# Longer rows in the prelude, one chain of side work for context keys and values, and full-width output units in a hybrid backbone layer

## The chip, the cores and the metric

The kernel runs on one core of one Trainium2 chip. The metric is the device time of one execution in microseconds (us); the time of a version is the median over its runs. The profile is of one execution and has its own time.

## The reference

One layer of a bidirectional backbone: 1024 latent tokens `x` and 256 context tokens `ctx`, width 2048, float32. Both are normalised and modulated with vectors computed from `c` and `c_ctx`, projected by `w_in` (10256 columns) and go through two groups of heads: eight HGRN2 heads (gated linear recurrence) and four mLSTM heads (matrix memory, with a short convolution on queries and keys). The context's final states seed the latent's scans.

```python
mod_x = silu(c) @ w_mod + b_mod                  # 3 sections: shift, scale, gate
mod_c = silu(c_ctx) @ w_mod + b_mod
u_ctx = modulate(ctx, shift_c, scale_c) @ w_in
y_ctx, ctx_states = mix(u_ctx, False, states0, *lp)   # only the states are used
u_x = modulate(x, shift_x, scale_x) @ w_in
y_x, _ = mix(u_x, True, ctx_states, *lp)
x = layer_norm(ALPHA * x + gate_x * (y_x @ w_out), ln_g, ln_b)
```

## The kernel before

Every product of the projections is taken with both factors split into a rounded part and a rest (`hi`, `lo`), so that one product is three matmuls, `xh·hi`, `xh·lo` and `xl·hi` (`mm3`, L222-232). ScalarE (ACT) makes `whi` from the loaded `wraw`, VectorE (DVE) makes `wlo` (L217, L218; in the deep ring of the last output groups L201, L202). SyncE's queue (SP) brings the weights.

The program is written as one stream of projection units, with side work in generators. After some 24 matmuls a unit calls `tick()` (L73), which moves each generator on by one step, to its next `yield`; a `yield n` asks for n ticks until the next step. `finish` (L81) runs a generator to its end on the spot. So a generator's steps stand in TensorE's instruction order between the matmuls of the units, and what is not stepped through by ticks stands in a row behind them. A matmul that waits holds up all behind it on its engine.

The stages that matter here:

- **Prelude** (L301-354). The shift and scale sections of `w_mod` are taken in eight eighths of 256 columns. `adaln_cols` (L356) loads each as eight tiles `am_raw` of two k-tiles, two transfers each with rows of 1 KB (L366), and multiplies with a stationary operand of 32 columns that fills one of four column groups (`o = 32 * (k % 4)`, L372), all in one PSUM bank. The sums are copied to `mod_rows` (L375), gathered with `comb` (L382) and added to the bias (`modc`); `ln_kp` (L431) transposes two k-tiles of the normalised context (L439) and modulates them. Between the eighths stand the context projections of keys and values of mLSTM heads 0 to 2, two k-tiles at a time, 256 columns a head. Six PSUM banks hold them until the end.
- **Context phase** (`phase_ctx`, L582). The context's gates (L588, L589), keys 3 and values 3, then for each pair of HGRN2 heads forget gates forward and backward and the input (`ctx_unit`). Side work: `ctx_k` (convolution over padded copies, transposes L673), `ctx_v`, `ctx_f` (decayed keys `c_kd` L722, each followed at once by its transposes L726), `ctx_i`, and normalising the latent tokens in four quarters (`lat_load`, `lat_gen`). The third and fourth quarters share their buffers (`hh1*`, `hl1*`) with the context, so they come after the last context projection, together with the latent gates (`gates_mm`, L575, L576) and three early mLSTM units.
- **mLSTM and HGRN2 heads**, some 2000 us, which the change hardly touches.
- **Output** (`phase_out`, `out_group` L1250). The heads' results go through DRAM (`d_y`) and are read back as `yh`, `yl` by GpSimd's queue (POOL, L1244). Row tiles of 128 tokens are taken in three groups, 4 + 2 + 2. A unit is 1024/n columns wide: 256 for the first group, 512 for the others. `evac` multiplies a finished bank with the gate (L1274), adds `ALPHA` times a piece of `x` that POOL loaded (L1275) and takes statistics (L1276). `out_norm` normalises a group and stores it from ACT's queue (L1320). Four row buffers `res` serve all groups. The PSUM pools (five `pj`, two `mx` and one `mx3` banks) are open from the start to the end, so output matmuls of the first unit are placed among the last head's instructions.

Of the kernel before, what the change touches and what calls it, by code (L numbers as in the profile page):

```python
# [38 lines left out]
class Body:  # L39
# [46 lines left out]
    def run(self):  # L86
        tc = self.tc
        with tc.tile_pool(name="const", bufs=1) as self.cp, \
                tc.tile_pool(name="hts", bufs=1) as self.hp, \
                tc.tile_pool(name="wts", bufs=1) as self.wp, \  # L90
                tc.tile_pool(name="psp", bufs=5, space=PSUM) as self.psp, \
                tc.tile_pool(name="psm", bufs=2, space=PSUM) as self.psm, \
                tc.tile_pool(name="dr", bufs=1, space=DRAM) as self.dp:
            self.setup()
            with tc.tile_pool(name="wgp", bufs=1) as self.gp:
                with tc.tile_pool(name="ph1a", bufs=1) as self.mp:
                    self.prelude()
                with tc.tile_pool(name="ph1", bufs=1) as self.mp:
                    self.phase_ctx()
            with tc.tile_pool(name="ph2", bufs=1) as self.mp:  # L100
                self.phase_mlstm()
            with tc.tile_pool(name="ph3", bufs=1) as self.mp:
                self.phase_hgrn()
            with tc.tile_pool(name="ph4", bufs=1) as self.mp:
                self.phase_out()


    def setup(self):
# [3 lines left out]
        nc.gpsimd.dma_start(out=self.comb, in_=a["k_comb"])  # L112
# [71 lines left out]
    def weights(self, src, cols, k0, nk, deep=False, ahead=True, pool=None):  # L184
# [3 lines left out]
        with self.tc.high_priority() if ahead else nullcontext():  # L188
# [15 lines left out]
            if pool is None:  # L204
                raw = self.wp.tile([P, nk, wd], F32, tag="wraw", bufs=2, name=self.nm("wraw"))
            else:
                raw = pool.tile([P, nk, wd], F32, tag="praw", bufs=6, name=self.nm("wraw"))
# [81 lines left out]

    def cht(self, k):  # L290
# [10 lines left out]
    def prelude(self):  # L301
# [3 lines left out]
        with self.tc.high_priority():  # L305
            nc.scalar.dma_start(out=cr[0:16], in_=a["c"].rearrange("o (r p) -> (o r) p", p=P))
            nc.scalar.dma_start(out=cr[16:32], in_=a["c_ctx"].rearrange("(r p) -> r p", p=P))
            nc.scalar.dma_start(out=self.ident, in_=a["k_ident"])
# [8 lines left out]

        self.wg = self.gp.tile([P, 16, 32], F32R, name="wg")
        gr = mp.tile([P, 16, 16], F32, name="wg_raw")
        nc.scalar.dma_start(out=gr, in_=a["w_in"][:, CG:CG + 16].rearrange("(k p) n -> p k n", p=P))  # L320
        hi, lo = self.wg[:, :, 0:16], self.wg[:, :, 16:32]
        nc.scalar.copy(hi, gr)
        nc.vector.tensor_tensor(out=lo, in0=gr, in1=hi.bitcast(F32), op=ALU.subtract)
        units = [self.pj([P, 2, 256]) for _ in range(5)]
        units.append(self.psm.tile([P, 2, 256], F32, tag="mx3", bufs=1, name=self.nm("mx")))
        rows = self.adaln_cols(0, ch)
        self.vectors()

        self.hth, self.htl = [None, None], [None, None]
        self.cth = [self.hp.tile([P, 2, 256], F32R, tag=f"hh1{k}", name=self.nm("cth")) for k in range(8)]  # L330
        self.ctl = [self.hp.tile([P, 2, 256], F32R, tag=f"hl1{k}", name=self.nm("ctl")) for k in range(8)]
        xa = []
        for i in range(2):
            xt = [self.hp.tile([P, 1024], F32, tag=f"hh0{i * 2 + s}", name=self.nm("cx")) for s in range(2)]
            for s in range(2):
                nc.scalar.dma_start(out=xt[s], in_=a["ctx"][i * P:(i + 1) * P, s * 1024:(s + 1) * 1024])
            self.ln_norm(xt)
            xa.append(xt)
        for e in range(9):
            if 0 < e < 8:  # L340
                rows = self.adaln_cols(e, ch)
            for h in range(3 if e else 0):
                k0 = 2 * e - 2
                parts = self.weights(a["w_in"], [(CMK + h * 256, 256), (CMV + h * 256, 256)], k0, 2, ahead=False,
                                     pool=mp)
# [1051 lines left out]
```

## Time and profile before

| | |
|---|---|
| median of 3 runs | 2912.41 us (2912.31 to 2923.12) |
| the profiled execution's own time | 2913.54 us |
| its span | 2911.7 us |
| mean granted TensorE clock | 0.989 of full |
| TensorE, VectorE, ACT, POOL busy | 97%, 53%, 32%, 13% of the span |

The span is the stretch that the profile covers; the own time of that execution is 1.8 us longer. "PE" is TensorE, "PEclk" the share of its full clock that was granted; "idle before, releaser" names what ended the idle time ahead of an instruction on its engine. The time bought or lost on an engine other than TensorE shows only where TensorE waits for it.

### The profile page before, as it was taken

What the parts mean: (1) busy time and instruction counts of PE and PEld (TensorE: products, weight loads), DVE (VectorE), ACT (ScalarE), POOL (GpSimd) and SP (SyncE); (2) the same over time, 40 slices, a digit from 0 to 9 for tenths busy, and PEclk for the clock granted to TensorE, in tenths of its full rate; (3) what the DMA queues carried; (4) which work ended last, traced back from release to release, by engine and by line L of the source; (5) the groups of instructions that cost most, each with busy time, mean ns of one, the idle gap of its engine ahead of it and who ended that gap; (6) DMA issues with size and microseconds to landing.
All of it is one profiled execution on the core that took longest, in us unless ns stands there. A gap on an engine that the chain in (4) does not pass through costs nothing.

```text
span 2911.7 us, 47253 instructions
## 1 busy us (share of the span) xinstructions
PE 2823.9 (97%) x19337; PEld 2408.6 (83%) x19337; DVE 1543.7 (53%) x3017; ACT 931.6 (32%) x1654; POOL 368.4 (13%) x550
## 2 busy tenths in 40 slices
PE   6899999999999999999999999999999999999998
PEld 3798976988887898789778888888888888899876
DVE  3387657563835655474625352534435353544776
ACT  1275446341233123222323231323223232322332
POOL 1011011031112103201310101011010101310111
PEclk9999999999999999999999999999999999999999
DMA  9945642124223322332241111121111212853784
GB/s 331 348 153 167 190 120 73 50 55 116 80 64 82 109 73 72 103 94 77 62 115 48 53 45 54 44 60 53 45 54 44 61 37 60 256 183 120 243 301 172
DMA packets 331960, 325.12 MB, mean 112 GB/s; under 512 B 16640, under 2 KB 285216, under 8 KB 329696
## 3 DMA queue, kind: packets, MB, share of 16 engines
q1 hardware_dynamic: 296976, 243.04, 27.8%
q0 software_dynamic: 30336, 69.15, 8.2%
q10 hardware_dynamic: 4432, 9.91, 0.9%
q8 instruction: 152, 2.49, 0.3%
q14 instruction: 64, 0.52, 0.1%
HBM read 289.00 MB, written 33.05 MB: 111 GB/s over the span
## 4 chain that ended last, share of the span: by engine, by line
PE 73%; DVE 4%; issue 2%; DMA 2%; POOL 1%; ACT 1%; DVEq 0%; POOLq 0%; ACTq 0%; SPq 0%
PE pj L226 16%; PE pj L228 16%; PE pj L227 16%; PE pj L230 5%; PE pj L232 5%; PE pj L231 5%; PE mx L1108 2%; PE mx L951 1%; PE mx L956 1%; PE mx L1189 1%; DVE m_acc L862 1%; PE mx L949 1%; DMA yl<-d_y 1%; DMA m_bc<-d_rows 1%; POOL m_rs L938 0%
## 5 line engine op out<-in xcount | busy, mean ns | idle before, releaser
L226 PE MATMUL pj<-hh,whi 128*128 128x512 f32 x2304 | 923.5, 401 | 0.7 <-ACT m_pad L784 0.7
L228 PE MATMUL pj<-hh,wlo 128*128 128x512 f32 x2304 | 900.6, 391 | 0.0
L227 PE MATMUL pj<-hl,whi 128*128 128x512 f32 x2304 | 899.6, 390 | 0.0
L218 DVE TENSOR_TENSOR wlo<-wraw,whi 128x512 fp32r<-128x512 f32 x556 | 390.4, 708 | 669.4 <-ACT whi L217 561.8
L217 ACT CAST whi<-wraw 128x512 fp32r<-128x512 f32 x556 | 340.3, 619 | 861.1 <-PE pj L227 533.5
L228 PEld LDWEIGHTS pj<-hh,wlo 128*128 128x128 f32 x2304 | 433.0, 188 | 93.2 <-issue 0.4
L226 PEld LDWEIGHTS pj<-hh,whi 128*128 128x128 f32 x2304 | 433.3, 188 | 92.7 <-issue 2.5
L227 PEld LDWEIGHTS pj<-hl,whi 128*128 128x128 f32 x2304 | 433.6, 188 | 86.5
L230 PE MATMUL pj<-whi,yh 128*128 128x256 f32 (+1 forms) x768 | 245.9, 320 | 4.4 <-DVE res L1274 4.4
L231 PE MATMUL pj<-wlo,yh 128*128 128x256 f32 (+1 forms) x768 | 245.6, 320 | 0.0
L232 PE MATMUL pj<-whi,yl 128*128 128x256 f32 (+1 forms) x768 | 245.4, 320 | 0.1
L862 DVE SCALAR_TENSOR_TENSOR m_acc<-m_pad,cwt,m_acc 128x512 f32<-128x512 f32 x256 | 188.6, 750 | 3.5
L230 PEld LDWEIGHTS pj<-whi,yh 128*128 128x128 f32 x768 | 147.0, 191 | 15.0 <-DVE res L1274 4.8
L232 PEld LDWEIGHTS pj<-whi,yl 128*128 128x128 f32 x768 | 146.9, 191 | 10.4 <-DMA yl<-d_y 0.3
L231 PEld LDWEIGHTS pj<-wlo,yh 128*128 128x128 f32 x768 | 146.9, 191 | 10.2
L230 PE MATMUL pj<-whi,hh 128*128 128x256 f32 x512 | 147.2, 287 | 0.9 <-ACT m_pad L784 0.9
L232 PE MATMUL pj<-whi,hl 128*128 128x256 f32 x512 | 144.9, 283 | 0.0
L231 PE MATMUL pj<-wlo,hh 128*128 128x256 f32 x512 | 144.8, 283 | 0.0
L1220 POOL TENSOR_TENSOR h_ss<-h_ss,nhalf 128x4 f32<-128x4 f32 x16 | 16.6, 1036 | 804.0 <-DVE h_ss L1219 804.0
L228 PE MATMUL pj<-cth,wlo 128*128 128x256 f32 x384 | 112.4, 293 | 5.3 <-DVE wlo L218 5.3
L1092 ACT COPY h_km<-h_kk 128x512 f32<-128x512 f32 x112 | 74.6, 666 | 125.9 <-DVE h_kk L1145 98.4
L226 PE MATMUL pj<-cth,whi 128*128 128x256 f32 x384 | 114.6, 298 | 0.0
(313 smaller groups left out, 3937.9 us busy)
## 6 DMA issues: line engine op xcount, KB each, us to landing
wraw<-in_w_in_dram SPq DMA_DIRECT2D x222, 512.0 KB, 3.8
wraw<-in_w_out_dram SPq DMA_DIRECT2D x96, 512.0 KB, 4.3
am_raw<-in_w_mod_dram SPq DMA_DIRECT2D x128, 256.0 KB, 6.0
wraw<-in_w_mod_dram SPq DMA_DIRECT2D x32, 512.0 KB, 3.6
d_y<-yhl POOLq DMA_DIRECT2D x64, 256.0 KB, 3.9
wraw<-in_w_in_dram SPq DMA_DIRECT2D x48, 256.0 KB, 6.0
xt<-in_x_dram SPq DMA_DIRECT2D x8, 1024.0 KB, 6.7
m_bc<-d_rows POOLq DMA_DIRECT2D x64, 128.0 KB, 3.4
```

Source lines behind the costliest of these rows:

```text
L217: nc.scalar.copy(hi, r)
L218: nc.vector.tensor_tensor(out=lo, in0=r, in1=hi.bitcast(F32), op=ALU.subtract)
L226: mm(o, hi, xh, start=start, stop=False, skip_group_check=True)
L227: mm(o, hi, xl, start=False, stop=False, skip_group_check=True)
L228: mm(o, lo, xh, start=False, stop=stop, skip_group_check=True)
L230: mm(o, xh, hi, start=start, stop=False, skip_group_check=True)
L231: mm(o, xh, lo, start=False, stop=False, skip_group_check=True)
L232: mm(o, xl, hi, start=False, stop=stop, skip_group_check=True)
L862: V.scalar_tensor_tensor(out=acc, in0=src, scalar=wc, in1=acc, op0=ALU.mult, op1=ALU.add)
L949: nc.tensor.matmul(po[:, 0:257], w, v1[:, c, :], start=True, stop=False)
L1092: nc.scalar.copy(view(km, 0, [[2 * B, 512 // (2 * B)], [B, 2], [1, B]]), view(kk, g * 512, [[2 * B, 512 // (2 * B)], [T + B, 2], [1, B]]))
L1108: nc.tensor.matmul(p3[q0:q0 + TW, c, :], kms[c // 4][:, cc + q0:cc + q0 + TW], rhs(c * P, j), start=True, stop=True, skip_group_check=True)
```

## The change

**Prelude.** The sections are taken in four quarters of 512 columns. A tile `am_raw` holds one k-tile of both sections, so its rows are 2 KB. A quarter is four groups `g` of four k-tiles (`adaln_mm`); within a group `j` is the column group, and the two sections go to two PSUM banks. Each of the quarters 1 to 3, and a fifth round without loads, has a context step (`ctx_first`) behind each group: keys of all four heads for one k-tile (24 matmuls) and values of heads 0 and 1, 512 columns wide (6 matmuls). Small loads (`ident`, the context, the gates' weights) move from ACT's queue to POOL's. The context rows now lie in one half of the buffers of latent quarters three and four.

**Context phase.** The four finished key banks are copied to `c_sk` at once and convolved from there without pads. Keys and values of heads 0 and 1 and keys 2 and 3 are one chain. Values 2 and 3 are one unit of 512 columns at the third head pair (`ctx_pair`). Latent quarters two and three and the load of four are one chain among the head pairs, and only `lat_gen(3)` comes behind them. `ctx_f` makes both decayed keys, then yields, then transposes both.

**Output.** All units are 512 wide. The heads' PSUM pools close first and the output has a pool of eight banks. `res` is loaded with whole rows of `x` by ACT's queue; `evac` writes `res = ALPHA * res + p * gb` through a tile `o_t`. The scratch memory of POOL's transfers is halved (8192 to 4096 bytes).

The core of the diff:

```diff
+        for e in range(5):
+            ps = [self.mx() for _ in range(2)] if e < 4 else None
+            for g in range(4):
+                if e < 4:
+                    self.adaln_mm(e, g, ch, ps)
...
+                if e:
+                    self.ctx_first(e * 4 - 4 + g)
+                if g == 3 and e < 4:
+                    self.adaln_mod(e, ps)
+                    for kp in (2 * e, 2 * e + 1):
+                        self.ln_kp(xa, kp, 1, self.cth[kp], self.ctl[kp])
+
+    def adaln_mm(self, e, g, ch, ps):
+        for j in range(4):
+            k = g * 4 + j
...
+            raw = self.hp.tile([P, 2, 512], F32, tag=tag, name=self.nm("am_raw"))
             for sec in range(2):
+                c0 = sec * D + e * 512
+                nc.sync.dma_start(out=raw[:, sec, :], in_=a["w_mod"][k * P:(k + 1) * P, c0:c0 + 512])
+            for sec in range(2):
+                nc.tensor.matmul(ps[sec][j * 32:j * 32 + 32, :], ch[:, k, :], raw[:, sec, :],
+                                 start=(g == 0), stop=(g == 3), skip_group_check=True)
...
+    def ctx_first(self, k):
+        raw = mp.tile([P, 3, 512], F32, tag="praw", bufs=4, name=self.nm("praw"))
...
+        for i in range(3):
...
+            for j in range(2):
+                if i < 2:
+                    s = slice(j * 256, (j + 1) * 256)
+                    self.ctx_mm(self.first_k[i * 2 + j], "a", hi[:, s], lo[:, s], k)
+                else:
+                    s = slice(j * P, (j + 1) * P)
+                    self.mm3(self.first_v[j], hi, lo, xh[:, s], xl[:, s], k == 0, k == KT - 1, False)
...
+        sk = mp.tile([P, 4, 2, NC], F32, name="c_sk")
+        for h in range(4):
+            nc.scalar.copy(sk[:, h], self.first_k[h])
+        self.mx3 = True
+        kv = self.side(self.chain([g], *[self.ctx_k(h, sk[:, h]) for h in (0, 1)],
+                                  *[self.ctx_v(h, self.first_v) for h in (0, 1)],
+                                  *[self.ctx_k(h, sk[:, h]) for h in (2, 3)]))
...
-        self.ctx_unit("a", CMK + 3 * 256, k_done(3))
-        self.ctx_unit("b", CMV + 3 * 256, v_done(3))
...
                 lat = [self.side(self.chain([], self.lat_load(1, xa[1]), self.lat_gen(1, xa[1]),
-                                            self.lat_load(2, xa[2])))]
+                                            self.lat_load(2, xa[2]), self.lat_gen(2, xa[2]),
+                                            self.lat_load(3, xa[3])))]
+            if h == 4:
+                more = []
+                self.ctx_pair(CMV + 512, lambda ps: more.append(
+                    self.side(self.chain([kv], *[self.ctx_v(h, ps) for h in (2, 3)]))))
...
-        lat = self.side(self.chain([], self.lat_gen(2, xa[2]), self.lat_load(3, xa[3]), self.lat_gen(3, xa[3])))
+        lat = self.side(self.lat_gen(3, xa[3]))
...
             kd = mp.tile([P, NC], F32, tag="c_kd", bufs=2, name=self.nm("c_kd"))
-            V.tensor_scalar(out=kd, in0=f, scalar1=-1.0, scalar2=1.0, op0=ALU.mult, op1=ALU.add)
-            V.tensor_tensor(out=kd, in0=kd, in1=ex, op=ALU.mult)
+            V.scalar_tensor_tensor(out=kd, in0=f, scalar=1.0, in1=ex, op0=ALU.subtract, op1=ALU.mult)
+            kds.append(kd)
             yield
+        for j in range(2):
             pt = self.mx()
...
-        wd = 1024 // n
-        nu = D // wd
+        wd, nu = 512, D // 512
+        for i in range(n):
+            nc.scalar.dma_start(out=res[i], in_=a["x"][(t0 + i) * P:(t0 + i + 1) * P, :])
...
-                V.tensor_tensor(out=rv, in0=p, in1=gb, op=ALU.mult)
-                V.scalar_tensor_tensor(out=rv, in0=xs[:, i, :], scalar=ALPHA, in1=rv, op0=ALU.mult, op1=ALU.add)
+                t = mp.tile([P, wd], F32, tag="o_t", bufs=2, name=self.nm("o_t"))
+                V.tensor_tensor(out=t, in0=p, in1=gb, op=ALU.mult)
+                V.scalar_tensor_tensor(out=rv, in0=rv, scalar=ALPHA, in1=t, op0=ALU.mult, op1=ALU.add)
...
-                tc.tile_pool(name="psp", bufs=5, space=PSUM) as self.psp, \
-                tc.tile_pool(name="psm", bufs=2, space=PSUM) as self.psm, \
...
+            with tc.tile_pool(name="ph4", bufs=1) as self.mp, \
+                    tc.tile_pool(name="pso", bufs=8, space=PSUM) as self.psp:
                 self.phase_out()
```

The order of the instructions, at three places. On TensorE in the prelude, one eighth before: `am_raw` is a tile of the modulation weights, `mx` the PSUM bank, `cx` the context rows; the matmuls ahead of these rows are context projections.

```order
L372 MATMUL mx_433<-am_raw_434,c_pad_116 32x512 x2
L372 MATMUL mx_433<-am_raw_439,c_pad_116 32x512 x2
L372 MATMUL mx_433<-am_raw_444,c_pad_116 32x512 x2
...
L372 MATMUL mx_433<-am_raw_469,c_pad_116 32x512 x2
L382 MATMUL mx_581<-comb,mod_rows_474 128x2 x4
L439 MATMUL mx_587<-ident,cx_221 128x128
L439 MATMUL mx_587<-ident,cx_237 128x128
```

The same place of the changed kernel, the first two groups of the second quarter, with the context step between them cut short:

```order
L402 MATMUL mx_326<-am_raw_338,c_pad_115 32x512
L402 MATMUL mx_327<-am_raw_338,c_pad_115 32x512
L402 MATMUL mx_326<-am_raw_343,c_pad_115 32x512
L402 MATMUL mx_327<-am_raw_343,c_pad_115 32x512
L223 MATMUL mx_127<-hh_133,whi_351 128x256
...
L402 MATMUL mx_326<-am_raw_393,c_pad_115 32x512
L402 MATMUL mx_327<-am_raw_393,c_pad_115 32x512
```

Sixteen matmuls into one bank in a row have become groups of eight that alternate between two banks, with 30 matmuls of a context step between two groups.

On TensorE at the end of the last HGRN2 head, before: L1228 are the transposes of the last head's results, L230 to L232 the first output unit.

```order
L232 MATMUL pj_22493<-whi_22501,yl_22422 128x256
L230 MATMUL pj_22493<-whi_22501,yh_22421 128x256
L1228 MATMUL mx_22387<-ident,h_y_22370 128x128 x4
L231 MATMUL pj_22493<-wlo_22502,yh_22421 128x256
L232 MATMUL pj_22493<-whi_22501,yl_22422 128x256
...
L232 MATMUL pj_22494<-whi_22497,yl_22418 128x256
L1228 MATMUL mx_22400<-ident,h_y_22379 128x128 x4
L230 MATMUL pj_22494<-whi_22501,yh_22421 128x256
```

And of the changed kernel, where L1249 are the transposes and L227 the first output matmul:

```order
L1228 MATMUL mx_22069<-h_v_21377,h_sc_21403 128x128
L1229 MATMUL mx_22069<-h_S_22018,h_qq_21096 128x128
L1230 MATMUL mx_22069<-h_S_22020,h_qq_21096 128x128
L1249 MATMUL mx_22100<-ident,h_y_22083 128x128 x4
L1249 MATMUL mx_22113<-ident,h_y_22092 128x128 x4
L227 MATMUL pj_22213<-whi_22219,yh_22135 128x512
L228 MATMUL pj_22213<-wlo_22220,yh_22135 128x512
L229 MATMUL pj_22213<-whi_22219,yl_22136 128x512
```

The output matmuls that stood between the last head's instructions, 36 ahead of the second transposes, now come behind them.

On ACT at the start of the output in the changed kernel: L1007 rounds the last head's results for the store, L214 rounds output weights, L1279 is the load of `x`; the waits are on semaphores of DMA queues and engines, `DMASW` those of POOL's transfers.

```order
L1007 CAST yhl_22120<-yt_22118 128x512 [waits DVE_49,Activation_49]
L214 CAST whi_22291<-wraw_22285 128x512 [waits PE_49]
L214 CAST whi_22321<-wraw_22319 128x512 [waits DMAHW3_49,PE_49]
L1279 DMA res_22199<-in_x_dram 128x2048 [waits DMASW1_49,DMASW4_49,DMASW0_49,DMASW7_49,Activation_49,Pool_49]
L214 CAST whi_22325<-wraw_22319 128x512 [waits PE_49]
L214 CAST whi_22355<-wraw_22353 128x512 [waits DMAHW4_49,PE_49]
L1279 DMA res_22200<-in_x_dram 128x2048
```

The loads of `x` stand among the casts of the weights, and the first waits for four of POOL's transfers; before, the casts follow each other and the queue has no such load.

## Rows read from the trace of the kernel before

**Rows 1.** The profile's page: the span, and TensorE's busy time, share and instructions.

```profile
span 2911.7 us, 47253 instructions
...
PE 2823.9 (97%) x19337; PEld 2408.6 (83%) x19337; DVE 1543.7 (53%) x3017; ACT 931.6 (32%) x1654; POOL 368.4 (13%) x550
```

**Rows 2.** Windows, prelude: length, busy time by engine (instructions), PEclk, DMA share, GB/s.

```profile
100.00:120.00 20.00, 18.29 (x142) 15.24 (x142) 5.73 (x10) 4.38 (x8) 0.00 (x0) 0.91 1.10 348
...
140.00:160.00 20.00, 19.19 (x168) 16.70 (x160) 11.16 (x24) 9.60 (x18) 0.55 (x1) 1.00 0.41 125
```

**Rows 3.** Windows of the context phase.

```profile
166.40:446.00 279.60, 260.27 (x1862) 238.29 (x1861) 192.52 (x387) 144.28 (x276) 40.64 (x49) 0.98 0.52 154
420.00:447.00 27.00, 18.62 (x84) 10.84 (x83) 16.35 (x24) 11.02 (x22) 6.09 (x6) 0.94 0.14 38
180.00:200.00 20.00, 17.83 (x130) 17.03 (x129) 18.81 (x50) 13.33 (x25) 2.55 (x3) 0.91 0.47 138
```

**Rows 4.** Windows of the output stage.

```profile
2500.00:2520.00 20.00, 20.00 (x270) 15.97 (x269) 10.93 (x23) 9.61 (x19) 11.06 (x16) 1.00 1.28 380
2600.00:2620.00 20.00, 20.00 (x169) 20.00 (x168) 8.12 (x17) 4.96 (x8) 1.29 (x2) 1.00 0.33 112
2720.00:2740.00 20.00, 20.00 (x90) 16.55 (x89) 18.61 (x30) 9.97 (x10) 4.79 (x7) 1.00 0.76 261
2760.00:2780.00 20.00, 15.60 (x59) 12.38 (x58) 10.46 (x14) 3.39 (x4) 1.09 (x2) 0.83 0.98 397
```

**Rows 5.** TensorE's timeline, last gate matmul: start, length, instruction, count.

```profile
166.11 0.28 PE L589 MATMUL mx<-ctl,wg 128*32 128x256 f32 x1
```

**Rows 6.** DMA queues, 40:140 us, then 2780:2880 us: packets, MB, share of engines.

```profile
q1 hardware_dynamic: 35949, 34.65, 109.2%
...
q1 hardware_dynamic: 10288, 19.83, 56.6%
```

**Rows 7.** One group of the output, by form: busy, mean ns | idle.

```profile
L230 PE MATMUL pj<-whi,yh 128*128 128x512 f32 x256 | 100.7, 393 | 4.4 <-DVE res L1274 4.4
```

**Rows 8.** TensorE's timeline, one eighth, then two matmuls that arrive alone.

```profile
105.09 0.28 PE L232 MATMUL mx<-whi,ctl 128*128 128x256 f32 x1
105.30 3.64 PE L372 MATMUL mx<-am_raw,c_pad 128*32 128x512 f32 x32
109.78 1.05 PE L382 MATMUL mx<-comb,mod_rows 128*128 128x2 f32 x8 [0.84 <-DVE mod_rows L375]
110.70 0.64 PE L439 MATMUL mx<-ident,cx 128*128 128x128 f32 x4
...
113.17 0.41 PE L227 MATMUL pj<-ctl,whi 128*128 128x256 f32 x1
113.38 0.41 PE L228 MATMUL pj<-cth,wlo 128*128 128x256 f32 x1
...
35.80 1.05 PE L372 MATMUL mx<-am_raw,c_pad 128*32 128x512 f32 x4 [0.45 <-DMA am_raw<-in_w_mod_dram]
```

**Rows 9.** TensorE's waits over the span: us in total, times, longest.

```profile
PE mx L726 <- DVE c_kd L722: 9.0, 7, 3.0
...
PE pj L230 <- DVE res L1274: 4.4, 1, 4.4
...
PE mx L673 <- DVE c_k L663: 2.2, 1, 2.2
```

**Rows 10.** Timelines at the change of output groups, VectorE, then TensorE.

```profile
2772.17 1.29 DVE L1274 TENSOR_TENSOR res<-pj,o_gb 128x512 f32<-128x512 f32 x2 [7.13 <-DMA out_dram<-res]
...
2773.51 0.63 PE L231 MATMUL pj<-wlo,yh 128*128 128x512 f32 x1
2773.93 0.63 PE L232 MATMUL pj<-whi,yl 128*128 128x512 f32 x1
```

**Rows 11.** TensorE's timeline at the end of the last head.

```profile
2531.65 0.37 PE L230 MATMUL pj<-whi,yh 128*128 128x256 f32 x1
...
2533.71 0.63 PE L1228 MATMUL mx<-ident,h_y 128*128 128x128 f32 x4 [0.26 <-DVE h_ss L1219]
```

More of the change, by code (lines that the diff above doesn't have):

```diff
@@ L288, in ctx_unit, with ctx_pair @@
             self.tick()
+    def ctx_pair(self, c0, done):
+        ps = [self.pj([P, 512]) for _ in range(2)]
+        for kg in range(8):
+            parts = self.weights(self.a["w_in"], [(c0, 512)], kg * 2, 2)
+            for kk in range(2):
+                k = kg * 2 + kk
+                xh, xl = self.cht(k)
+                for j in range(2):
+                    s = slice(j * P, (j + 1) * P)
+                    self.mm3(ps[j], *parts[kk], xh[:, s], xl[:, s], k == 0, k == KT - 1, False)
+            if kg == 7:
+                done(ps)
+            self.tick()
     def cht(self, k):
@@ L316, in prelude @@
         nc.vector.tensor_copy(self.ccol, pc[:, 0:16])
[L318 to L331, printed above, removed]
         xa = []
@@ L335, in prelude @@
             for s in range(2):
[L336 to L337 removed]
+                nc.gpsimd.dma_start(out=xt[s], in_=a["ctx"][i * P:(i + 1) * P, s * 1024:(s + 1) * 1024])
             xa.append(xt)
[L339 to L345, printed above, removed]
[L346 to L353 removed]
@@ L354, in prelude @@
-        self.first = units
-    def adaln_cols(self, e, ch):
-        nc, a, mp = self.nc, self.a, self.mp
-        ps = self.mx()
-        for kp in range(8):
+        self.first_k = [self.psm.tile([P, 2, 256], F32, tag="mx3", bufs=1, name=self.nm("mx"))]
+        self.first_k += [self.pj([P, 2, 256]) for _ in range(3)]
+        self.first_v = [self.pj([P, 512]) for _ in range(2)]
+        self.hth, self.htl = [None, None], [None, None]
+        self.alloc_ht(1)
+        self.cth = [t[:, :, 256:512] for t in self.hth[1]]
@@ L374, in adaln_cols @@
-        rows = mp.tile([P, 512], F32, tag="mod_rows", bufs=2, name=self.nm("mod_rows"))
-        nc.vector.tensor_copy(rows, ps)
-        return rows
-    def adaln_mod(self, e, rows):
-        nc = self.nc
-        pc = self.mx()
-        for j in range(4):
-            nc.tensor.matmul(pc[:, j * 2:j * 2 + 2], rows[:, j * P:(j + 1) * P], self.comb,
-                             start=True, stop=True)
-        dst = self.modc[:, :, 2 * e:2 * e + 2, :]
-        nc.vector.tensor_tensor(out=dst, in0=pc[:, 0:8].rearrange("p (c j s) -> p c j s", j=2, s=2),
-                                in1=view(self.colv1, 2 * e, [[16, 2], [1, 2], [0, 2]]), op=ALU.add)
+                c0 = sec * D + e * 512
```

193 lines of the change are left out of this document (90 added, 103 removed).

## The prediction

> **What bounds the kernel.** The page first: TensorE is busy for 97% of the 2911.7 us span [rows 1]. So time can be won only where TensorE waits, runs at the lower clock, or does avoidable work. The windows say where. From 40 to 140 us the DMA share is 1.1 of the 16 engines at 348 GB/s, while at 140:160 it is 0.41 [rows 2]: the prelude is bound by its loads. Of 180:200 TensorE leaves 2.2 us idle, of 420:447 8.4, and the granted clock is below full in both [rows 3]. In the output stage it is full except at 2760:2780, with 15.6 of 20 at a clock of 0.83 [rows 4]. Between, from about 505 to 2520 us, the order of TensorE's work hardly changes: 41 rows of 8338 differ. I cost that stretch at nothing; its cover is TensorE's own full load.
>
> **Part A, the prelude: -10 us.** It ends with the context gate matmuls at 166.4 us [rows 5]. *Loads.* The bytes stay; the rows double from 1 KB to 2 KB. The prelude's queue, on 1 KB rows, takes 109.2% of 16 engines for 34.65 MB in 100 us, 50.4 engine-us per MB [rows 6]. Output weights in 2 KB rows take 56.6% for 19.83 MB, 45.7 per MB [rows 6]. At full share, 348 x 50.4/45.7 = 384 GB/s (estimate). Ahead of the last modulation weights lie about 45.6 MB (33.55 of modulation weights, 2.1 of context, 12 of 16 loads of 0.79 MB, small ones); with a start at 1.9 us these land at 1.9 + 45.6/0.384 = 121 us. Then follow the last modulation group (2.0), its transposes, five context steps (21) and the gates (32 of 0.115, 3.7): 152. The transposes are a wait for the rows of 0.84, the 1.05 of today's eight passes doubled and the 0.64 of today's four transposes doubled [rows 8]: 4.2.
>
> *TensorE.* A context step is 24 matmuls of 256 columns and 6 of 512. Spacing comes from counts: 20/169 = 0.118 us and 20/90 = 0.222 us in full windows [rows 4], not from a mean such as 393 ns for 512 columns, whose matmuls overlap [rows 7]. A step is 24 x 0.12 + 6 x 0.222 = 4.2 us, 16 steps 67. A modulation group is 8 matmuls, 16 passes. Today 32 passes run as one burst in 3.64 us, 0.114 each, because four column groups work side by side [rows 8]: 1.8 us, and I take 2.0 with the changes between column groups and whole array. The row after 105.09 starts 0.21 later rather than 0.12 [rows 8], so a change costs about 0.1 each way. On this the Trainium skill (TensorEngine Tiling, Key Properties) says that changing the tiling mode drains TensorE, which speaks against 16 short groups in place of 8 bursts; the trace agrees that something is paid, but at 0.1 us it adds 2 us in all and is in the 2.0. The chain: first quarter's weights and transposes until 38 (loads of 11 MB at 348 to 384, then 4 to 5), 12 groups 24, 16 steps 67, three transposes 13, four clock falls 7 (one in 100:120, where matmuls stand 0.21 apart at 113 [rows 8]; the granted 0.91 of 20 us [rows 2] is 1.8), gates 3.7: 153. Both chains end at 152 to 153 and hinder each other, so I say 156, -10. Bounds: best, neither hinders the other, -15; worst, groups in pairs that don't overlap, passes of 0.43 (worked below), +13.
>
> **Part B, context phase: -17 us.** From 166.4 to 446 us TensorE is busy for 260.3 of 279.6 us [rows 3]: 19 idle. *Waits.* The two transposes of a decayed key now follow both vector chains and a tick of 24 matmuls (2.9 us): of the 9.0 us in seven waits [rows 9] I take 6. Keys are read in place, without pads, and come two ticks ahead: 2.2 of 2.2 [rows 9]. *Third quarter.* Today it begins when the context rows are free, after the projections, with too few ticks over it: 420:447 is busy for 18.62 of 27 us [rows 3]. Now its eight steps and its loads run among the head pairs' ticks, and only the fourth quarter's eight are left for about 14 ticks: 8 of the 8.4 idle. Its clock fall goes too: 0.06 of 27 us, 1.6. *Values 2 and 3* by 512 columns: 192 x 0.12 = 23.0 against 96 x 0.222 = 21.3: 1.7. *New.* The first quarter has fewer ticks over it since keys 3 and values 3 left: 14 steps on 12, about two uncovered, +4 with one clock fall. VectorE is busy for 18.8 of 20 us there [rows 3] and loses pads and memsets: nothing either way, if it gains a load TensorE waits as now. Sum -15.5, or -19.5 if the new two steps find cover; I take -17. Bounds: -25 (all idle goes) and -8 (only the third quarter's).
>
> **Part C, output: -12 us.** *Width.* The first group issues 1536 matmuls of 256 columns, 0.1183 apart, 181.7 us; now 768 of 512, 0.222 apart, 170.5 [rows 4]: -11.2. *The stall.* TensorE stops for 4.4 us at 2768.5 because a first-of-unit matmul waits for a bank that VectorE empties at 2772.17 [rows 9, 10]; VectorE had stood 7.13 us for an output store, because the new group's rows reuse the stored groups' buffers. Behind it 12 matmuls run 0.43 apart instead of 0.222 [rows 10], 2.6 us lost. Now eight banks, four units of 96 x 0.222 = 21 us, lie before a bank is needed; VectorE still waits for the store and the load, but TensorE does not: -4.4 - 2.6 = -7.0. Seven weight subtractions stand ahead of that wait on VectorE, so weights for 7 x 2.67 (12 of 0.222) = 19 us are there. *Lost cover.* The pools of the heads close before the output opens its own, so the 36 output matmuls that stand among the last head's now come behind it. Today they fill the chain from 2531.65 past the two groups of transposes [rows 11]: 36 x 0.118 = 4.2 uncovered, plus a clock fall of 1.8: +6. Bounds 0 (the next work covers it) to +9 (the first output weights are late too). *New on ACT:* x is loaded by ACT, whose first load waits for four stores of the last head's rows. Casts queue behind it; before them two are done and five buffers of 2.67 us lie ready, against some 10 us: nothing, and at worst +8. The evacuation's two-step form is the same two VectorE instructions. A halved ring for POOL's transfers is bounded by 0 and +3; I take 0, since the first output unit uses the 8.4 MB that the ring brings it over 43 us. Sum -12.2; I take -12. Bounds -18 (full cover) to +2 (all three ends).
>
> **Sum.** -10 - 17 - 12 = -39 against this execution's own 2913.54 us (1.8 of it outside the span, left as they are): 2874.5. The median of the runs, 2912.41, is 1.1 lower, so **2873**.
>
> **The rivals.** *1. The loads don't speed up.* At 348 GB/s the weights land at 1.9 + 45.6/0.348 = 133, the prelude ends at 164, A is -2.8: **2881**. For it: 100 us lie flat at 348 [rows 2]. Against: 2 KB rows cost a tenth less engine time [rows 6], and 380 GB/s passed from 2500 to 2520 [rows 4]. Chance 0.10. The Trainium skill (DMA: Bandwidth & Descriptors, Where 436 GB/s comes from) says that for transfers between HBM and SBUF about 358 per core binds; by that the end would be at 160, A -6; the trace's 380 disagrees.
>
> *2. Column groups overlap only in part.* Each group now sends two sections to the same column group in a row. If the second holds back the next column group, a group costs about twice as much, 4.2 us: 12 x 2.2 = 26 more, prelude 179, A +12.5: **2896**. Against: two matmuls that arrive alone still run their 4 passes in 1.05 us, not 4 x 0.43 = 1.7 [rows 8]. Chance 0.10.
>
> *3. Slower: the groups run one after the other.* Between context steps each matmul waits for the one ahead: 16 x 0.43 = 6.9 us a group. TensorE's chain is then 153 + 12 x 4.9 = 212, A +45, and the sum **2928**. It decides once a group exceeds 6.6 us (12 x 4.6 = 55 more, and since the two chains begin level, all of A, B and C is gone). Against, as for 2. Chance 0.06.
>
> *4. The early third quarter only moves its waits*, VectorE being full at 180:200 [rows 3]: B is -8, **2882**, inside the range; counted with the forecast.
>
> **How the numbers follow.** Forecast 0.74 (with 4), rivals 0.10, 0.10, 0.06. A measurement here tells about 0.5% from no change, 14.6 us: faster is below 2897.8, slower above 2927. The forecast's own bounds, A -15 to -2, B -25 to -8, C -18 to +2, sum to -58 and -8, 2855 and 2904, and seldom fall together; 2855 to 2890 holds nearly all of it. The range keeps the low end, a little under it for the prelude's unseen rate, and reaches past rivals 1 and 2: 2852 to 2900. Faster: 0.74 + 0.10 + most of 0.10, less for bounds that fall together, 0.87; same 0.07; slower 0.06.
>
> **What would show it.** The last gate matmul at 150 to 160 us with over 370 GB/s in the windows from 40 to 100; modulation groups of 2 us; no wait above 1 us on decayed keys; TensorE full in the stretch ahead of the latent gates, which is 420:447 now; no stall of TensorE at the change of output groups, but some 4 us idle after the last head's transposes. A prelude that ends after 170, a stop of TensorE behind ACT's x loads, or a middle that differs by more than 3 us would make me wrong.

## The result, and the profile after

The changed kernel takes **2884.86 us** in the median of four runs (2884.11 to 2890.44). Its ratio to the kernel before on the same chip is **0.9892**, with an interval from 0.9876 to 0.9908: 27 to 36 us less. The forecast was 2873 in a range of 2852 to 2900, 39 us less. The sign and the range hold; the gain is about three quarters of what I summed.

The profiled execution is the longest of the four, 2890.44 us with a span of 2888.6. A second set of runs of the same kernel gave 2883.0 to 2888.0, its profiled one 2888.0. The stage times below come from the two profiles; they hold for executions that are some 2 to 6 us longer than the median.

| end of the stage, start of its last matmul (us) | before | after | after, second profile | forecast for the stage |
|---|---|---|---|---|
| prelude: last context gate matmul | 166.1 | 157.4 (-8.8) | 156.2 (-10.0) | -10 |
| last state matmul of the last head | 2531.6 | 2518.0 (-4.8 more) | 2515.0 (-6.6 more) | -17 |
| end of the span | 2911.7 | 2888.6 (-9.5 more) | 2886.2 (-8.9 more) | -12 |

The prelude and the output came close. The context phase is where 10 us of the forecast are missing. The second row holds this phase and the heads: from the last context gate matmul to the last latent one it takes 279.5 us before, 275.6 and 272.1 after; from there to the last state matmul 2086.1, 2085.0 and 2086.7, so the middle hardly moves, as forecast. Nine output matmuls of the kernel before, 1.1 us, stand ahead of its last state matmul and none of the changed kernel's, so 1.1 us of the second row's gain belong to the third.

The profile's page of the changed kernel: the span and section 1, which answer to [rows 1].

```profile
span 2888.6 us, 45096 instructions
...
PE 2816.8 (98%) x18377; PEld 2356.4 (82%) x18377; DVE 1528.7 (53%) x2913; ACT 933.8 (32%) x1657; POOL 362.0 (13%) x552
```

Its windows (columns as in [rows 2]): the prelude, the context phase, the output.

```profile
100.00:120.00 20.00, 20.00 (x138) 14.69 (x139) 8.23 (x14) 6.52 (x13) 0.00 (x0) 0.91 1.05 389
...
166.40:446.00 279.60, 261.51 (x1746) 232.71 (x1746) 184.58 (x340) 144.13 (x277) 45.86 (x69) 0.98 0.53 153
420.00:447.00 27.00, 26.28 (x110) 17.43 (x109) 8.42 (x13) 7.99 (x13) 2.89 (x7) 1.00 0.31 84
...
2760.00:2780.00 20.00, 19.45 (x86) 15.83 (x85) 9.04 (x10) 4.58 (x5) 0.54 (x1) 1.00 1.00 405
```

Against [rows 2] the loads run at 389 GB/s in place of 348. Against [rows 3] the stretch 420:447 is full, 26.28 of 27, as forecast; yet the whole phase from 166.4 to 446 has 18.1 us of idle TensorE, where it had 19.3. Against [rows 4] the stop at the change of output groups is gone: 19.45 of 20 us at a clock of 1.00.

### The profile page after: what moved, and what is told of

Read it like the earlier page. It is cut to its first block, busy times and chain, and to the rows that moved or that the text cites. A ratio compares the mean times of both kernels' runs of the same rounds, so it can differ in the third digit from the quotient of the medians.

```text
span 2888.6 us, 45096 instructions
## 1 busy us (share of the span) xinstructions
PE 2816.8 (98%) x18377; PEld 2356.4 (82%) x18377; DVE 1528.7 (53%) x2913; ACT 933.8 (32%) x1657; POOL 362.0 (13%) x552
## 4 chain that ended last, share of the span: by engine, by line
PE 71%; DVE 4%; DMA 3%; issue 2%; ACT 1%; POOL 1%; DVEq 0%; ACTq 0%; POOLq 0%; SPq 0%
PE pj L223 16%; PE pj L225 16%; PE pj L224 16%; PE pj L228 5%; PE pj L227 5%; PE pj L229 5%; DMA wraw<-in_w_out_dram 2%; PE mx L1129 2%; PE mx L972 1%; PE mx L977 1%; PE mx L1210 1%; PE mx L970 1%; PE mx L904 1%; DVE res L1335 1%; PE mx L1229 0%
## 5 line engine op out<-in xcount | busy, mean ns | idle before, releaser
L223 PE MATMUL pj<-hh,whi 128*128 128x512 f32 (+1 forms) x2656 | 1027.9, 387 | 1.0 <-ACT m_pad L805 0.7
L224 PE MATMUL pj<-hl,whi 128*128 128x512 f32 (+1 forms) x2656 | 1001.9, 377 | 0.0
L225 PE MATMUL pj<-hh,wlo 128*128 128x512 f32 (+1 forms) x2656 | 1000.5, 378 | 1.0 <-DVE wlo L215 1.0
L214 ACT CAST whi<-wraw 128x512 fp32r<-128x512 f32 x508 | 311.7, 619 | 788.5 <-PE pj L224 544.3
L227 PE MATMUL pj<-whi,hh 128*128 128x256 f32 (+1 forms) x704 | 210.9, 300 | 1.7 <-ACT m_pad L805 1.4
L228 PE MATMUL pj<-wlo,hh 128*128 128x256 f32 (+1 forms) x704 | 207.4, 295 | 2.1 <-DVE wlo L215 2.1
L229 PE MATMUL pj<-whi,hl 128*128 128x256 f32 (+1 forms) x704 | 207.1, 294 | 0.0
L227 PE MATMUL pj<-whi,yh 128*128 128x512 f32 x512 | 200.1, 391 | 0.8 <-DVE yt L1003 0.8
L228 PE MATMUL pj<-wlo,yh 128*128 128x512 f32 x512 | 200.3, 391 | 0.6 <-DVE wlo L202 0.6
L229 PE MATMUL pj<-whi,yl 128*128 128x512 f32 x512 | 199.9, 390 | 0.0
L228 PEld LDWEIGHTS pj<-wlo,hh 128*128 128x128 f32 x704 | 135.6, 193 | 5.4 <-DVE wlo L215 3.6
L227 PEld LDWEIGHTS pj<-whi,hh 128*128 128x128 f32 x704 | 135.6, 193 | 5.4 <-ACT m_pad L805 1.6
L227 PEld LDWEIGHTS pj<-whi,yh 128*128 128x128 f32 x512 | 96.5, 189 | 21.2 <-DVE yt L1003 1.1
```

What stands on the lines that cost most here:

```text
L214: nc.scalar.copy(hi, r)
L223: mm(o, hi, xh, start=start, stop=False, skip_group_check=True)
L224: mm(o, hi, xl, start=False, stop=False, skip_group_check=True)
L225: mm(o, lo, xh, start=False, stop=stop, skip_group_check=True)
L227: mm(o, xh, hi, start=start, stop=False, skip_group_check=True)
L228: mm(o, xh, lo, start=False, stop=False, skip_group_check=True)
```

## The experiments

Twelve runs follow. Each expectation stands as it was recorded.

**The same kernel again.**

> The changed kernel unaltered, for a second profile. Its profiled execution took 2890.44 us, its other three 2884.1 to 2885.1. If those 5.6 us are chance of one execution, the new profile shows a span near 2883 and the missing 5 us lie in one stage between the two profiles. If the profiled execution is always longer, it is again about 2890 with the same stage times.

Measured: 2885.6 us (2883.0 to 2888.0), ratio 0.9894 (0.9876 to 0.9912), span of the profile 2886.2. The second profile is 4.7 us ahead at the last latent gate matmul (428.3 against 433.0), 1.2 of it from the prelude, and 2.4 at the end. The window of 160:450 (columns as in [rows 2]), first profile, then second:

```profile
160.00:450.00 290.00, 271.91 (x1807) 240.39 (x1806) 193.41 (x356) 149.75 (x287) 46.58 (x70) 0.98 0.53 152
160.00:450.00 290.00, 271.71 (x1817) 240.23 (x1816) 196.45 (x360) 153.42 (x291) 47.01 (x70) 0.99 0.52 152
```

TensorE is idle for 18.1 and 18.3 us, the same; what differs is the granted clock. The first has three stretches of 10 us at 0.83 (from 180, 230 and 330), the second one at 0.85 (from 330), and the means, 0.982 and 0.994 over 290 us, make the 3.5 us by which this phase differs. So the idle time of one profile is not the whole price of a version. Executions of this kernel differ by some 5 us; differences of less between two versions are not read as such below.

**The output part alone, in the kernel before.**

```diff
-        wd = 1024 // n
+        wd, nu = 512, D // 512
...
+            with tc.tile_pool(name="ph4", bufs=1) as self.mp, \
+                    tc.tile_pool(name="pso", bufs=8, space=PSUM) as self.psp:
```

> The kernel before with the output part of the change alone (512 columns throughout, pools closed before the output, eight banks, x by ACT's queue). My forecast for this part was -12 against before, about 2901 to 2903. The stages of the two profiles give -9.5, about 2904. If the part works only together with the others (less load at the same time), it gives less than -6.

Measured: 2905.31 us, ratio 0.9969 (0.9956 to 0.9982), so 9 us less (5 to 13). From the last head's last state matmul to the last output matmul (start to start) it takes 357.1 us, the changed kernel 356.6, the kernel before 366.0. The part works by itself.

**The third quarter put back.**

```diff
-                                            self.lat_load(2, xa[2]), self.lat_gen(2, xa[2]),
-                                            self.lat_load(3, xa[3])))]
+                                            self.lat_load(2, xa[2])))]
...
-        lat = self.side(self.lat_gen(3, xa[3]))
+        lat = self.side(self.chain([], self.lat_gen(2, xa[2]), self.lat_load(3, xa[3]), self.lat_gen(3, xa[3])))
```

> The changed kernel with its third latent quarter put back behind the context projections. My forecast: the early quarter saves 8 us and a clock fall there, so this is slower than the changed kernel by 8 to 10, about 2893 to 2895. The rival: the early quarter only moves its waits into 180 to 340 us, where VectorE is nearly full; then this is within 3 us of the changed kernel, 2882 to 2888, with less idle time of TensorE in 200 to 340 and 8 us more behind it.

Measured: 2885.77 us, ratio 0.9901 (0.9884 to 0.9919), against 2885.6 for the changed kernel in the same set: no difference that can be told. Windows of 280:340 and 360:450, first of the kernel before, then of the changed kernel, then of this one:

```profile
280.00:340.00 60.00, 56.15 (x451) 55.27 (x450) 43.91 (x84) 30.32 (x60) 6.51 (x8) 0.97 0.63 193
360.00:450.00 90.00, 80.90 (x452) 62.92 (x449) 45.29 (x73) 37.78 (x69) 15.64 (x19) 0.98 0.37 106
```

```profile
280.00:340.00 60.00, 51.44 (x380) 48.61 (x381) 47.75 (x87) 31.43 (x61) 10.91 (x14) 0.97 0.62 179
360.00:450.00 90.00, 89.28 (x487) 69.71 (x487) 37.44 (x59) 36.57 (x66) 9.59 (x14) 1.00 0.39 104
```

```profile
280.00:340.00 60.00, 58.83 (x455) 56.60 (x455) 35.22 (x68) 26.67 (x57) 6.04 (x13) 1.00 0.63 173
360.00:450.00 90.00, 80.55 (x393) 60.12 (x394) 47.15 (x73) 37.00 (x67) 15.81 (x20) 0.96 0.34 99
```

Subtract the first busy time, TensorE's, from the length. With the late quarter TensorE is idle for 1.2 and 9.5 us, with the early one for 8.6 and 0.7. The 8.7 us behind the projections are gained, and 7.4 of them are paid back among the head pairs. That was rival 4, which I had left inside the forecast.

**The transposes of the decayed keys one tick later.**

```diff
             kds.append(kd)
-            yield
+            yield 1 + j
```

> The changed kernel with the transposes of the decayed keys put off by one more tick (24 matmuls, 2.9 us). If those waits (8.5 us in four, the longest 3.3, each with a clock fall behind it) are only lateness of 2 to 3 us, they vanish: 8 to 13 us less than the changed kernel, 2872 to 2877. If VectorE's load as a whole is the bound there, the waits come back on weights or on other transposes and the time is within 3 us of the changed kernel.

Measured: 2888.42 us, ratio 0.9911 (0.9894 to 0.9928): nothing gained. TensorE's waits from 160 to 450 us, in the changed kernel:

```profile
PE mx L746 <- DVE c_kd L740: 8.5, 4, 3.3
PE mx L746 <- ACT h_raw L482: 2.5, 3, 1.8
PE pj L228 <- DVE wlo L215: 2.1, 4, 1.3
PE mx L471 <- DVE xt L461: 1.4, 1, 1.4
```

and with the later transposes:

```profile
PE mx L746 <- DVE c_kd L740: 4.9, 2, 2.8
PE mx L708 <- ACT h_raw L482: 3.2, 2, 1.8
PE mx L746 <- ACT h_raw L482: 2.7, 1, 2.7
PE mx L471 <- ACT c_kdt L748: 2.2, 2, 1.6
```

The wait on the keys (L746 are the transposes of [rows 9], now behind both keys) falls from 8.5 to 4.9, but 5.4 us stand on L708 and L471 for a `mx` bank that ACT has to read, where the changed kernel has 1.2. The idle time as a whole falls from 18.1 to 15.8 us and the total does not. So the waits are not lateness of one chain.

**Modulation weights in rows of 1 KB, half the size.**

```diff
-                nc.sync.dma_start(out=raw[:, sec, :], in_=a["w_mod"][k * P:(k + 1) * P, c0:c0 + 512])
+                for q in range(2):
+                    nc.sync.dma_start(out=raw[:, sec, q * 256:(q + 1) * 256],
+                                      in_=a["w_mod"][k * P:(k + 1) * P, c0 + q * 256:c0 + (q + 1) * 256])
```

> The changed kernel with the modulation weights in rows of 1 KB again (twice as many transfers of half the size), all else as changed. If the prelude is bound by its loads, as my forecast has it, the rate falls from 385 to about 350 GB/s, the last gate matmul comes at about 163 instead of 157 us, and the time is 5 to 7 us above the changed kernel (2890 to 2892). If TensorE's own chain binds the prelude, it stays within 2 us of the changed kernel.

Measured: 2930.03 us, ratio 1.0043 (1.0028 to 1.0058), the last gate matmul at 200.5 us, the queue at 272 GB/s from 40 to 140. The expectation missed: the edit also doubled the number of transfers, and their issue became the bound. SP's queue in this run:

```profile
40.02 7.77 SPq L401 DMA_DIRECT2D am_raw<-in_w_mod_dram  x16
```

Sixteen transfers of 128 KB in 7.77 us are 0.49 us each, 270 GB/s, while the DMA engines' share from 40 to 120 us is 0.88, where the changed kernel has 1.04. It shows that the prelude follows its loads, not what row length does; hence the run with transfers of 256 KB below.

**Eight banks, with the heads' pools left open.**

```diff
-        banks = [self.pj([P, wd]) for _ in range(n)]
+        banks = [self.bank() for _ in range(n)]
...
+    def bank(self):
+        self.nbank = getattr(self, "nbank", -1) + 1
+        i = self.nbank % 8
+        if i < 5:
+            return self.pj([P, 512])
+        tag, bufs = ("mx", 2) if i < 7 else ("mx3", 1)
+        return self.psm.tile([P, 512], F32, tag=tag, bufs=bufs, name=self.nm("mx"))
```

with `run` as in the kernel before.

> The changed kernel with the heads' PSUM pools left open to the end; the output takes the five, two and one banks of the three tags in turn, so it still has eight banks, but its first matmuls can stand among the last head's again. By my account the closed pools cost 6 us at the last head (waits of 1.9 and 1.6, and 2.6 of lower clock and wait behind): 5 to 7 us below the changed kernel, 2878 to 2880, the last transposes without a wait above 0.5. If something else holds the first output matmuls (their weights or the stores of the last head), it is the same as the changed kernel.

Measured: **2878.42 us** (2876.2 to 2882.2), ratio 0.9870 (0.9855 to 0.9885), the fastest version. The changed kernel's TensorE at the end of the last head:

```profile
2520.11 0.63 PE L1249 MATMUL mx<-ident,h_y 128*128 128x128 f32 x4 [1.81 <-DVE h_ss L1240]
2522.27 0.63 PE L1249 MATMUL mx<-ident,h_y 128*128 128x128 f32 x4 [1.53 <-ACT yhl L1007]
2523.74 0.64 PE L227 MATMUL pj<-whi,yh 128*128 128x512 f32 x1 [0.84 <-DVE yt L1003]
2524.17 0.63 PE L228 MATMUL pj<-wlo,yh 128*128 128x512 f32 x1
...
2528.17 0.39 PE L227 MATMUL pj<-whi,yh 128*128 128x512 f32 x1
...
2530.44 0.39 PE L228 MATMUL pj<-wlo,yh 128*128 128x512 f32 x1
```

and with the pools open (L1248 are the same transposes, L226 the first output matmul):

```profile
2506.53 0.47 PE L226 MATMUL pj<-whi,yh 128*128 128x512 f32 x1
...
2519.47 0.63 PE L1248 MATMUL mx<-ident,h_y 128*128 128x128 f32 x4 [0.19 <-DVE h_ss L1239]
2521.79 0.60 PE L1248 MATMUL mx<-ident,h_y 128*128 128x128 f32 x4
```

Waits of 1.81, 1.53 and 0.84 us and the matmuls 0.43 apart behind them are gone; from the last state matmul to the last output matmul it takes 349.0 us in place of 356.6. Five output matmuls, 1.1 us, now stand ahead of that state matmul, so some 6.5 of the 7.6 us are won, as the medians say (6.4). The lost cover of the forecast's Part C is real, and it did not have to be lost.

**Latent rows loaded three ticks ahead.**

```diff
-        for j in range(2):
-            xt = mp.tile([P, D], F32, tag="xt", bufs=2, name=self.nm("xt"))
+        xts = [mp.tile([P, D], F32, tag="xt", bufs=2, name=self.nm("xt")) for _ in range(2)]
+        for j, xt in enumerate(xts):
             r0 = i * 256 + j * P
             nc.sync.dma_start(out=xt, in_=self.a["x"][r0:r0 + P, :])
+        if i:
+            yield 3
+        for j, xt in enumerate(xts):
             self.ln_norm([xt])
```

> The changed kernel with the loads of latent quarters two to four issued three ticks before VectorE takes their statistics. In the changed kernel VectorE stands 7 us in 180 to 340 us at the head of such a statistic until the load lands, with decayed keys queued behind it. If that is what keeps TensorE's waits on decayed keys at 8 to 10 us, they fall by 3 to 6, and with a clock fall or two the time is 3 to 8 us below the changed kernel, 2877 to 2882. If VectorE's work as a whole is the bound, it is within 2 us.

Measured: 2886.78 us, ratio 0.9896 (0.9879 to 0.9912). VectorE's standing for the rows falls from 7.1 to 2.8 us and TensorE's idle time from 160 to 450 us from 18.1 to 15.9, but the total does not move.

**The rests of the latent rows on POOL.**

```diff
-        (nc.vector if which or kp % 2 else nc.gpsimd).tensor_tensor(out=lo, in0=raw, in1=hi.bitcast(F32), op=ALU.subtract)
+        (nc.vector if which else nc.gpsimd).tensor_tensor(out=lo, in0=raw, in1=hi.bitcast(F32), op=ALU.subtract)
```

> The changed kernel with all subtractions that split the latent rows on POOL, which takes 16 of 0.69 us from VectorE over the phase (12 of them in 180 to 340 us, 8 us of 160) and gives POOL 16 more of some 1.3. If VectorE's work as a whole is the bound in 180 to 340 us, TensorE's waits there fall by about a third, 3 to 6 us below the changed kernel. If only the order on VectorE matters, within 2 us; slower by 2 or 3 if the latent gates now wait for POOL.

Measured: 2894.21 us, ratio 0.9921 (0.9907 to 0.9936): slower than the changed kernel by some 8 us. It relieved VectorE by less than it took over: from 180 to 340 us VectorE is busy for 122.1 us in place of 127.2. Groups by form from 180 to 340 us, of the changed kernel, then of this run:

```profile
L215 DVE TENSOR_TENSOR wlo<-wraw,whi 128x512 fp32r<-128x512 f32 x76 | 55.9, 747 | 17.1 <-ACT whi L214 16.6
...
L484 POOL TENSOR_TENSOR hl<-h_raw,hh 128x512 fp32r<-128x512 f32 x12 | 16.4, 1368 | 39.4 <-ACT hh L483 39.3
```

```profile
L215 DVE TENSOR_TENSOR wlo<-wraw,whi 128x512 fp32r<-128x512 f32 x74 | 59.9, 823 | 28.3 <-ACT whi L214 28.3
...
L484 POOL TENSOR_TENSOR hl<-h_raw,hh 128x512 fp32r<-128x512 f32 x24 | 32.2, 1345 | 41.9 <-ACT hh L483 38.5 <-DVE c_acc L672 3.3
```

With twice the subtractions on POOL each of VectorE's own takes 823 ns in the mean in place of 747, and VectorE stands 28.3 us for ACT's casts in place of 16.6. What makes the total 8 us longer was not tried apart.

**Latent rows by POOL's queue**, in the version with eight banks open.

```diff
-            nc.sync.dma_start(out=xt, in_=self.a["x"][r0:r0 + P, :])
+            nc.gpsimd.dma_start(out=xt, in_=self.a["x"][r0:r0 + P, :])
```

> The version with eight banks open (2878.4 us in its runs), with the latent rows loaded by POOL's queue in place of SP's. In the changed kernel ACT stands 49 us (33 before) in 160 to 345 us for weights; two loads of 1 MB stand ahead of them on SP's queue at each quarter, 6.3 us at 322. If these late weights are what keeps TensorE waiting in 280 to 340 us, its idle time there (some 8 us) halves: 3 to 5 us below, 2873 to 2875. If VectorE is the bound, within 2 us.

Measured: 2886.85 us, ratio 0.9907 (0.9891 to 0.9922): 8 us slower than its base. The edit did not bring the weights earlier: ACT's standing for them from 160 to 345 us, in the base and then in this run:

```profile
ACT whi L213 <- DMA wraw<-in_w_in_dram: 47.1, 28, 6.0
ACT whi L213 <- DMA wraw<-in_w_in_dram: 53.4, 27, 5.3
```

So it does not settle whether late weights hold TensorE; it shows that taking the rows off SP's queue does not bring the weights earlier.

**Modulation wholly on ACT**, in the same version.

```diff
-            if kk == 0:
+            if kk == 0 and which:
                 nc.vector.tensor_scalar(out=raw[:, kk, :], in0=src, scalar1=sc, scalar2=sh,
```

> The version with eight banks open (2878.4 us), with both halves of the latent rows modulated on ACT, which takes 24 of 0.53 us, 12.8 in all, from VectorE in 180 to 340 us without work for POOL; ACT is busy for 10 to 13.5 of 20 us there. If VectorE's work as a whole is the bound, TensorE's idle time in 180 to 340 us (16 to 17 us) falls by a third to a half and the time by 5 to 8 us, 2870 to 2873. If the order or the loads are the bound, within 2 us; slower if ACT now holds the weights' casts.

Measured: 2883.85 us (2880.9 to 2888.5), ratio 0.9896 (0.9879 to 0.9914), 5 us above its base where 5 to 8 below were expected. The window of 180:340, in the base and then in this run:

```profile
180.00:340.00 160.00, 142.37 (x1024) 132.54 (x1024) 129.23 (x245) 89.25 (x179) 31.59 (x45) 0.98 0.61 181
180.00:340.00 160.00, 143.63 (x1029) 133.26 (x1028) 117.96 (x222) 97.12 (x202) 30.89 (x46) 0.98 0.60 180
```

VectorE has 11.3 us less work, and TensorE is idle for 16.4 us in place of 17.6. So VectorE's load alone is not the bound. But ACT has 7.9 us more, and VectorE now stands for ACT's casts for 24.5 us in place of 15.6; that ACT took over as what holds TensorE is not excluded.

**Rows of 1 KB, transfers of 256 KB.** A tile now holds two k-tiles of one section, loaded as two halves of 256 columns; the matmuls keep the changed order.

```diff
-                nc.sync.dma_start(out=raw[:, sec, :], in_=a["w_mod"][k * P:(k + 1) * P, c0:c0 + 512])
+                for q in range(2):
+                    nc.sync.dma_start(out=raw[:, :, q * 256:(q + 1) * 256],
+                                      in_=a["w_mod"][k * P:(k + 2) * P, c0 + q * 256:c0 + (q + 1) * 256]
+                                      .rearrange("(k p) n -> p k n", p=P))
```

> The changed kernel with the modulation weights in rows of 1 KB but transfers of 256 KB as before and after (two k-tiles by 256 columns), the matmuls in their changed order. The run with transfers of 128 KB was held by their issue, 0.49 us each on SP's queue. If the length of the rows sets the rate, it is 348 to 355 GB/s from 40 to 120 us, the last gate matmul comes 5 to 7 us later (163) and the time is 2890 to 2892. If the size of the transfers or the free ACT queue made the rate, it stays at 385 and within 2 us of the changed kernel.

Measured: 2893.89 us, ratio 0.9929 (0.9913 to 0.9944). Window 40:120 of the changed kernel, then of this run, and this run's last gate matmul:

```profile
40.00:120.00 80.00, 75.96 (x526) 54.13 (x528) 28.27 (x51) 24.75 (x47) 0.00 (x0) 0.96 1.04 385
40.00:120.00 80.00, 76.45 (x512) 52.47 (x509) 27.12 (x53) 25.73 (x48) 0.00 (x0) 0.94 1.08 361
```

```profile
162.68 0.28 PE L628 MATMUL mx<-hl,wg 128*32 128x256 f32 x1
```

361 GB/s at a share of 1.08 in place of 385 at 1.04, and the prelude ends 5.3 us later than in the changed kernel's profile. The length of the rows sets the rate, and at 361 the rate sets the end of the prelude. At 385 the two chains end level: the last modulation weights land at 124.8 us, and TensorE, busy for all of 100:120, comes to them at 125.2. That the rate is a little above 355 is put down to the context weights, which keep their long rows; this was not tried. The median lies 9 us above the changed kernel's, the expectation was 5 to 7; where the rest lies is not known.

**Three edits together**: the three diffs above for later transposes, loads ahead and modulation on ACT, in the version with eight banks open.

> The version with eight banks open (2878.4 us), with three edits at once that did not pay one by one: the transposes of the decayed keys one tick later, the latent rows loaded three ticks ahead, and their modulation wholly on ACT. If several queues stand side by side and each alone is enough to hold TensorE in 180 to 340 us, taking all three away brings its idle time there from 16 to below 8 us and the time to 2866 to 2872. If something that none of them touches sets it (the few PSUM banks of the side work, or the order in which the side work is issued), the idle time stays at 13 to 17 us and the time is within 3 us of 2878.

Measured: 2881.46 us (2876.3 to 2881.6), ratio 0.9877 (0.9857 to 0.9897): no better than its base of 2878.4. TensorE's waits from 160 to 450 us:

```profile
PE mx L710 <- ACT h_raw L481: 4.5, 2, 3.8
PE mx L748 <- DVE c_kd L742: 2.4, 1, 2.4
PE pj L224 <- DVE wlo L214: 2.2, 4, 1.2
```

The wait on the keys is down to 2.4 us, and the longest is now one of 3.8 us for a `mx` bank. The idle time from 160 to 450 us is 15.9 us, 18.7 in its base; from 180 to 340, the stretch of the expectation, it is 12.0 in place of 17.6, between what the two cases said.

## Why the prediction was right or wrong

**Part A (-10) was right in its mechanism and, with some luck, in its sum.** 384 GB/s was estimated from two queues [rows 6], 385 measured from 40 to 120 us. A modulation group was put at 2.0 us; it takes 1.94. TensorE's timeline, two groups with a context step between:

```profile
106.19 1.94 PE L402 MATMUL mx<-am_raw,c_pad 128*32 128x512 f32 x16
112.53 1.94 PE L402 MATMUL mx<-am_raw,c_pad 128*32 128x512 f32 x16
```

The step is 6.34 - 1.94 = 4.4, against 4.2. So rivals 2 and 3 fall: two sections in the same column group cost nothing, as the 4 passes in 1.05 us had said [rows 8], and a group takes 0.1 us more than 16 passes of a long burst. The Trainium skill (TensorEngine Tiling, Key Properties) says that a change of the tiling mode drains TensorE; the trace agrees that no more than 0.1 to 0.2 us a group is paid for it. Rival 1 falls too; the Trainium skill's 358 GB/s (DMA: Bandwidth & Descriptors, Where 436 GB/s comes from) is passed for 80 us. The two runs with short rows show that the prelude follows its loads when these are slower. The luck: the last weights were to land at 121 us and land at 124.8 (46.6 MB moved by then, not 45.6, and the first 40 us ran at 331 and 363 GB/s). I had added 4 us because the two chains would hinder each other; SP waits for buffers that TensorE holds for only some 2 us in 0:130, and the late landing used up the 4.

**Part B (-17) failed, and it is the step that made the sum too large.** Up to the last head the profiles give -4.8 and -6.6; by the runs' ratio (31 us in all), less 10 for A and 9 for the output alone, it is some -12 at most. Rival 4's -8, with 2882, lies nearer than the forecast; the range held the result since it was wide enough for both. Two terms failed. "8 of the 8.4 idle" for the third quarter: that idle time went, but 7.4 us came back at 280 to 340, and the run without the move is as fast. I had read the price from the stage that the work leaves, and nothing from the one it enters. "Of the 9.0 us in seven waits I take 6": 8.5 us remain in four waits, and 2.5 more for banks at the same transposes. I had taken the distance of a tick for the whole delay; the run with one more tick shows that the wait then goes to another instruction. The 2.2 us on keys went too, and a wait on a decayed key took their place. Before, then after:

```profile
182.69 0.55 PE L673 MATMUL mx<-ident,c_k 128*128 128x128 f32 x3 [2.17 <-DVE c_k L663]
```

```profile
182.65 0.69 PE L746 MATMUL mx<-ident,c_kd 128*128 128x128 f32 x2 [2.47 <-DVE c_kd L740]
```

The +4 of the first quarter can't be told apart: idle time in 160:280 goes from 6.9 to 8.2. What sets the 16 to 18 us of idle time from 160 to 450 is not settled: one tick more, VectorE's standing, VectorE's work, and the queue of the latent rows were each changed, three edits at once, and none brought it below 15.8. In the runs with later transposes the waits that came up are for `mx` banks that ACT had still to read; that fits too few banks, or ACT as the bound, and neither was tried.

**Part C (-12) had its mechanisms right and its sizes a little off.** The stop of 4.4 + 2.6 us [rows 9, 10] went; from 2540 us on TensorE's longest wait is 0.6. The lost cover was put at +6; the waits of 1.81, 1.53 and 0.84 and the lower clock behind them (nine matmuls in 3.75 us, 1.7 more than at 0.227 each) are 5.9, against 0.4 there before, and the run with the pools open gains 6.4. The width was put at -11.2; from start to start a matmul of 512 columns takes 0.227 us (2528.17 to 2530.44 is ten of them) and one of 256 takes 0.120 (2531.97 to 2533.05 of the profile of before is nine), so it is 174 - 184 = -10. Counting instructions in a window of 20 us had counted those that hang over its edges [rows 4]. The three make -10 - 7 + 6.4 = -10.6; the table has -9.5 and -8.9, and -10.6 and -10.0 with the 1.1 us of its second row. ACT issues its first `x` load at 2534.52, 2.8 us after its last cast, and nothing on TensorE waits for it, as said.

## What to carry to other kernels

When side work is moved to an earlier stretch, price it at the place it enters: if TensorE already waits there for the same engines, the idle time moves along. Compare the granted clock of two profiles before their idle times: here it moved 3.5 us between two executions of one kernel. Closing a pool to get more buffers also closes the overlap across that border; taking the same banks in turn from the open pools kept both, 6 us here. Where a queue is full, long rows gain in proportion to the engine time per byte, which two queues of the profile of before already show.

## What was not expected of the hardware

- Splitting a transfer of 256 KB into two of 128 KB, with the same rows, turned a queue bound by bandwidth (348 to 361 GB/s) into one bound by issue: 0.49 us each on SP's queue, 272 GB/s at a share of 0.88.
- Twelve more subtractions on POOL within 160 us lengthened VectorE's own of the same kind from 747 to 823 ns, 74 x 0.076 = 5.6 us, against the 8.2 us taken from it. Its operations with one tensor input keep their length, 534 ns for `h_raw` and 392 for `c_f` in both runs; of those with two, `c_acc` goes from 601 to 683 and `c_kd` stays, 491 and 487. The Trainium skill (SBUF — State Buffer, SBUF: two separate sides) says that a VectorE operation with two SBUF inputs and a GpSimd operation that reads SBUF lock each other out, and the trace agrees in kind.
- Executions of one and the same program differ by 5 to 6 us here: 2884.1 to 2890.4 and 2883.0 to 2888.0 for the changed kernel. In the two that were profiled, the granted clock of the context phase is 0.982 and 0.994.
